# A macaron decoder block on one core: the order of each engine's instructions from the other of two scheduling models

## Chip, core and metric

The kernel runs on one NeuronCore of a Trainium2 chip. The metric is device time in microseconds of one launch; lower is better. A core has five instruction streams that run side by side and wait for each other through semaphores: PE (TensorE, matmuls), DVE (VectorE), ACT (ScalarE), POOL (GpSimd) and SP (SyncE, which only issues DMA transfers here). Each engine takes its own stream strictly in the order in which it was written into the program, so an instruction that waits holds up everything behind it on its engine.

## What is computed

One decoder layer of 1024 tokens and width 1024 in float32: a half-weight SwiGLU feed-forward block of width 2816, a mixer that merges gated linear attention (GLA, 4 heads) with gated DeltaNet (8 heads), and a second such feed-forward block; RMSNorm stands ahead of each and at the end.

```python
h = x
h = h + 0.5 * swiglu(rms_norm(h, ffn1_norm), w_gate1, w_up1, w_down1)
h = h + hybrid_mixer(rms_norm(h, mix_norm), ...)
h = h + 0.5 * swiglu(rms_norm(h, ffn2_norm), w_gate2, w_up2, w_down2)
out = rms_norm(h, final_norm)

# DeltaNet in the mixer, each head, over chunks of the sequence, one after the other:
def step(S, xs):
    qdc, qkc, uc, wc, kc, gc = xs
    v_new = uc - wc @ S
    o = qdc @ S + qkc @ v_new
    S = S * gc + kc.T @ v_new
    return S, o
```

The state S of a DeltaNet head goes from chunk to chunk, so the chunks of a head can't run side by side.

## The kernel before

**Stages.** Activations lie with features on the 128 partitions and the 1024 tokens along the free axis. The stages follow one another: the first feed-forward block (its norm, gate and up products in seven-product block form, then the down products), the mixer's DeltaNet heads, its GLA heads, the output product, the second feed-forward block, the last norm. By the trace the first gate and up products run to about 464 us, the down products to 640, the DeltaNet stage to about 1378, GLA to 1882, the output product and the start of the second feed-forward block to 2026, its gate and up products to 2406, its down products to 2568.

**Matmuls in float32.** Every large product is made of three matmuls on operands split into a high and a low part: high by ACT (a cast, L118 or L124), low by DVE (a subtraction, L119 or L125). `dense` (L137) takes a weight unit times 1024 tokens; `strassen` (L366) and `down` (L572) take block products, and several products accumulate into one PSUM bank, with DVE reading the bank in between (L577 in `down`, L377 in `strassen`).

**The start.** While the first products run, DVE computes the norm's factor ny (L202 to L206), which PE spreads over partitions (L211); and the block sums t2, t3 and t4 of the activations (L320, L327, L329, split at L125), which the fourth and fifth product of a `strassen` call need (L366 on t2h, t2l, t3h, t3l).

**A DeltaNet head.** `delta_rec` runs eight chunk steps, each a chain in which PE and DVE take turns, all on 128 x 128 tiles:

```python
nc.tensor.matmul(out=q[:, :P], lhsT=kT[:, c, :], rhs=S, ...)         # L1013
nc.vector.tensor_sub(out=r, in0=vt3[:, c, :], in1=q[:, :P])          # L1015
nc.tensor.matmul(out=q[:, :P], lhsT=yi3[:, c, :], rhs=r, ...)        # L1017
nc.vector.tensor_scalar(out=w, in0=q[:, :P], scalar1=cj[:, c:c + 1], ...)  # L1019
nc.tensor.matmul(out=oc, lhsT=w, rhs=qk3[:, c, :], ...)              # L1021
nc.tensor.matmul(out=oc, lhsT=S, rhs=qT[:, c, :], ...)               # L1023
nc.tensor.matmul(out=q[:, :P], lhsT=kst3[:, c, :], rhs=w, ...)       # L1026
nc.vector.scalar_tensor_tensor(out=s2, in0=S, scalar=gl[...], in1=q[:, :P], ...)  # L1031
```

After every fourth chunk the output is normed: ACT squares it (L1036), DVE adds (L1037), PE sums over partitions (L799), ACT takes a logarithm, an exponential and a square (L801 to L803, with two table loads), DVE finishes (L804, L805, L1039). Behind the last chunk of a head stands what the next head needs before its first L1017: transposes (L875), the products of k and q (L901), transposes of v (L962), and the levels of a blocked inverse (L980, L993), which PE, ACT and DVE take in turns; all read and write the four PSUM banks named q. Ahead of that, GpSimd has solved small triangles (L923, L926), and DMAs bring them back in blocks, xb and yb (L932 and in `delta_blocks`).

The projections of later heads (`project` through `dense`, L137, 128 x 512) are independent of this chain; each head brings 144 of them or more.

**What sets the order.** The program text only lists instructions and their data. At the end of the `with tile.TileContext(nc) as tc:` block the library's scheduler lays every engine's instructions out in a list of its own choice. It walks through the program with a timing model of the engines and places, at each point, what the model holds to be ready. The text gives it hints: `tc.high_priority(offset=400)` lifts an instruction ahead of others, `tc.issue_after(x)` keeps it behind x, and buffer counts of pools and PSUM banks bound how far ahead it may go.

Of the kernel before, what the change touches and what calls it, by code (L numbers as in the profile page):

```python
# [48 lines left out]
def tile_macaron_hybrid(  # L49
# [17 lines left out]
    nc = tc.nc  # L67
# [55 lines left out]
    def split(src, hi, lo, eng=None):  # L123
        a = nc.scalar.copy(out=hi, in_=src)  # L124
        b = (eng or nc.vector).tensor_sub(out=lo, in0=src, in1=hi.bitcast(F32))  # L125
        return a.ins, b.ins
# [134 lines left out]
    def block_units(blocks):  # L261
        base, units = 0, []
        for b in blocks:
            nd = 8 // len(b)
            units.append([(base + i, i * nd, nd) for i in range(KT // nd)])
            base += KT // nd
        return units
# [41 lines left out]
    def strassen_products(tp, xs, tmp, corner, raws, place=bank, pool_steps=3):  # L309
        comb = {}  # L310

        def tile512(n):
            return tp.tile([P, 512], F32, name=n, tag=n)

        def sums_own():
            for c in ("t2", "t3", "t4"):
                comb[c] = [tp.tile([P, 4, 512], F32R, name=c + p, tag=c + p) for p in "hl"]
            for k in range(4):
                def join(out, r, sl, eng):
                    eng.tensor_add(out=out, in0=xs[r][0][:, sl].bitcast(F32), in1=xs[r][1][:, sl].bitcast(F32))  # L320
                    return out

                b12 = join(corner(), k, HI, nc.vector)
                b22 = join(tile512("c11"), k + 4, HI, nc.vector)
                b11 = join(tile512("c21"), k, LO, nc.vector)
                b21 = join(tile512("c22"), k + 4, LO, nc.gpsimd)
                nc.vector.tensor_sub(out=b22, in0=b22, in1=b12)  # L327
                split(b22, *(x[:, k] for x in comb["t3"]))
                nc.vector.tensor_add(out=b11, in0=b11, in1=b22)  # L329
                split(b11, *(x[:, k] for x in comb["t2"]))  # L330
                nc.gpsimd.tensor_sub(out=b21, in0=b21, in1=b11)
                split(b21, *(x[:, k] for x in comb["t4"]), nc.gpsimd)

        def sums_inplace(k, tile):
            eng = nc.gpsimd if k < pool_steps else nc.vector
            hi, lo = xs[k][0][:, HI], xs[k][1][:, HI]
            v = tile(eng)
            eng.tensor_add(out=v, in0=lo.bitcast(F32), in1=hi.bitcast(F32))
            for t in xs[k]:
                eng.tensor_sub(out=v, in0=v, in1=t[:, LO].bitcast(F32))  # L340
            split(v, hi, lo, eng)

        def strassen(u0, u1, out, mid=None, early=False, begin=(None, None), last_sb=False):
            # Two weight units times x as a 2 x 2 block product (units x features, features x tokens) in the seven
            # products of Winograd's form of Strassen's scheme; those that follow one another in an output
            # accumulate in one bank. The sums of blocks are float32, split into hi and lo like any operand.
            srcs = ((u0, 0), (u0, 1), (u1, 0), (u1, 1))
            a11, a12, a21, a22 = raws()
            for t, (u, hf) in zip((a11, a12, a21, a22), srcs):
                nc.sync.dma_start(out=t, in_=u[:, hf * 512:hf * 512 + 512])  # L350

            def combine(o, a, b, op):
                with tc.high_priority(offset=400), tc.issue_after(norm_end[0]):
                    nc.gpsimd.tensor_tensor(out=o, in0=a, in1=b, op=op)  # L354
                return o

            def product(ps, w, xpart, first=False):
                wh = wp.tile([P, 512], F32R, name="wh", tag="wh")
                wl = wp.tile([P, 512], F32R, name="wl", tag="wl")
                with tc.high_priority(offset=400):  # L360
                    recent[:] = split(w, wh, wl)
                for k in range(4):
                    c = slice(k * P, k * P + P)
                    xh, xl = xpart(k)
                    for a, (p, q) in enumerate(((wh, xl), (wl, xh), (wh, xh))):
                        nc.tensor.matmul(out=ps, lhsT=p[:, c], rhs=q, start=(first and k == 0 and a == 0),  # L366
                                         stop=(k == 3 and a == 2), skip_group_check=not first)

            def keep(name, ps):
                t = tile512(name)  # L370
                with tc.high_priority(offset=400):
                    marks[0] = nc.scalar.copy(out=t, in_=ps).ins  # L372
                return t

            def add(t, ps):
                with tc.high_priority(offset=400):
                    marks[1] = nc.vector.tensor_add(out=t, in0=t, in1=ps).ins  # L377
                return t

            def part(r, sl):  # L380
                return lambda k: [t[:, sl] for t in xs[r + k]]

            def own(c):
                return lambda k: [t[:, k] for t in comb[c]]

            marks = [None, None]
            y = place()
            product(y, a11, part(0, LO), True)
            if begin[0]:
                begin[0]()  # L390
            c11 = keep("c11", y)
            q = place()
            product(q, a12, part(4, LO), True)
            if begin[1]:
                begin[1]()
            add(c11, q)
            out(0, LO, c11, q)
            s1 = combine(tmp(), a21, a22, ALU.add)
            combine(a21, a11, a21, ALU.subtract)
            combine(a11, s1, a11, ALU.subtract)  # L400
            combine(a12, a12, a11, ALU.subtract)
            if mid and early:
                mid(marks)
            product(y, a11, own("t2"))
            c21 = keep("c21", y)
            z = place()
            product(z, a21, own("t3"), True)
            c22 = keep("c22", z)
            if mid and not early:
                mid(marks)  # L410
            product(y, s1, part(0, HI))
            out(1, HI, add(c22, y), c22)
            product(z, a22, own("t4"))
            out(1, LO, add(c21, z), c21)
            product(y, a12, part(4, HI))
            if last_sb:
                out(0, HI, keep("c11", y), None)
            else:
                out(0, HI, y, tile512("c11"))

        return sums_own, sums_inplace, strassen
# [281 lines left out]
    with ExitStack() as st:  # L703
# [7 lines left out]
        units = block_units(OBLOCKS)[1]  # L711
# [733 lines left out]
```

## Time and profile before

| | |
|---|---|
| time, median of 3 | 2680.55 us (2671.61 to 2687.12) |
| span of the profiled execution | 2675.6 us |
| PE busy | 2510.3 us, 94% |
| DVE busy | 1871.0 us, 70% |
| ACT, POOL busy | 1066.7 and 1070.4 us, 40% each |
| mean granted clock of TensorE | 0.979 |

No separate time is listed for the profiled execution: its span, from first to last instruction, is 4.95 us below the median and stands for it. "Busy" of PE overlaps: a lone matmul is counted with its whole latency, so PE can look busier than the work it has. In the rows of single instructions the columns are start, duration, engine, line, operation, and result <- operands with shapes; a bracket at the end gives the idle time before the row and what ended it. [...]

### The profile page before, as it was taken

To read this page: it belongs to the slowest core of one execution; us is meant where nothing else is said; L and a number is where in the kernel's file an instruction comes from. 1 tells how busy PE (TensorE), PEld (TensorE's weight loads), DVE (VectorE), ACT (ScalarE), POOL (GpSimd) and SP (SyncE) were. 2 spreads that over 40 slices of the span, in tenths; PEclk is the share of its full clock that TensorE was granted. 3 is DMA by queue.
4 is the path that set the end of the run, shared out by engine and by line. 5 is a ranking of instruction groups with operands and counts; after the bars stand their busy time and mean duration, and the time that the engine had idled before them with its cause. 6 is when DMAs were issued, how large, how long until landed. Compare 5 with 4: busy or idle time off the path is not lost.

```text
span 2675.6 us, 32736 instructions
## 1 busy us (share of the span) xinstructions
PE 2510.3 (94%) x11656; PEld 2021.6 (76%) x11656; DVE 1871.0 (70%) x2907; ACT 1066.7 (40%) x1845; POOL 1070.4 (40%) x1136
## 2 busy tenths in 40 slices
PE   7899999899997998889989999999989999998998
PEld 6788888667776777767767787877768888886677
DVE  8755556999686777766596757767586555559996
ACT  5333334333352444444344544535233333343331
POOL 4544444653326344443352212221144544446531
PEclk9999999999998999999999999999999999999999
DMA  3222221322221222222211212122302222213222
GB/s 113 79 74 80 83 91 60 114 79 90 95 82 47 64 60 60 56 52 52 64 50 41 80 44 79 43 80 87 122 29 78 68 87 87 87 59 114 79 87 79
DMA packets 150819, 199.05 MB, mean 74 GB/s; under 512 B 69976, under 2 KB 76888, under 8 KB 150656
## 3 DMA queue, kind: packets, MB, share of 16 engines
q1 hardware_dynamic: 146192, 186.14, 22.0%
q0 software_dynamic: 2304, 8.39, 0.8%
q10 hardware_dynamic: 2160, 2.43, 0.3%
q8 instruction: 92, 1.51, 0.2%
q14 instruction: 71, 0.58, 0.1%
HBM read 158.73 MB, written 38.17 MB: 74 GB/s over the span
## 4 chain that ended last, share of the span: by engine, by line
PE 58%; DVE 16%; POOL 11%; issue 5%; ACT 4%; DMA 4%; SPq 2%; POOLq 0%; DVEq 0%; ACTq 0%
PE q L366 28%; PE m L366 10%; PE ps L137 8%; PE q L572 6%; POOL xp L926 5%; POOL itmp L923 4%; DVE wl L125 2%; DVE ha L577 1%; PE q L901 1%; DVE xl L125 1%; DMA lt<-l_d 1%; DVE h L577 1%; DMA raw<-in_win 1%; DMA s<-a_d 1%; SPq L932 1%
## 5 line engine op out<-in xcount | busy, mean ns | idle before, releaser
L125 DVE TENSOR_TENSOR wl<-raw,wh 128x512 fp32r<-128x512 f32 x244 | 199.7, 819 | 172.0 <-ACT wh L124 170.5
L137 PE MATMUL ps<-xl,wh 128*128 128x512 f32 (+2 forms) x736 | 256.8, 408 | 20.5 <-ACT wh L118 8.2
L125 DVE TENSOR_TENSOR wl<-sr,wh 128x512 fp32r<-128x512 f32 x232 | 204.1, 880 | 77.0 <-ACT wh L124 76.7
L137 PE MATMUL ps<-xh,wh 128*128 128x512 f32 (+2 forms) x736 | 254.4, 405 | 0.0
L137 PE MATMUL ps<-xh,wl 128*128 128x512 f32 (+2 forms) x736 | 254.1, 404 | 0.1
L366 PE MATMUL q<-xh,wl 128*128 128x512 f32 x640 | 250.0, 391 | 0.0
L366 PE MATMUL q<-xl,wh 128*128 128x512 f32 x640 | 249.4, 390 | 0.0
L366 PE MATMUL q<-xh,wh 128*128 128x512 f32 x640 | 249.0, 389 | 0.0
L124 ACT CAST wh<-sr 128x512 fp32r<-128x512 f32 x232 | 143.7, 619 | 244.2 <-PE q L572 62.1
L923 POOL TENSOR_TENSOR itmp<-lt,xp 128x112 f32<-128x112 f32 (+29 forms) x248 | 114.2, 461 | 292.7 <-DMA lt<-l_d 273.9
L124 ACT CAST wh<-raw 128x512 fp32r<-128x512 f32 x244 | 144.9, 594 | 175.7 <-PE q L366 101.0
L471 POOL TENSOR_TENSOR s<-s,ysc 128x512 f32<-128x512 f32 x80 | 112.2, 1414 | 248.0 <-ACT s L470 248.0
L137 PEld LDWEIGHTS ps<-xl,wh 128*128 128x128 f32 (+1 forms) x736 | 137.9, 192 | 51.1 <-DVE xl L237 9.0
L354 POOL TENSOR_TENSOR raw<-sr 128x512 f32<-128x512 f32 x20 | 26.4, 1322 | 331.3 <-DMA sr<-in_win 218.0
L137 PEld LDWEIGHTS ps<-xh,wl 128*128 128x128 f32 (+1 forms) x736 | 138.8, 192 | 24.6 <-issue 1.0
L137 PEld LDWEIGHTS ps<-xh,wh 128*128 128x128 f32 (+1 forms) x736 | 138.0, 192 | 24.4 <-issue 1.0
L377 DVE TENSOR_TENSOR c<-c,q 128x512 f32<-128x512 f32 x120 | 82.4, 687 | 85.4 <-PE q L366 85.4
L366 PEld LDWEIGHTS q<-xl,wh 128*128 128x128 f32 x640 | 120.1, 188 | 26.8 <-issue 0.3
L366 PEld LDWEIGHTS q<-xh,wl 128*128 128x128 f32 x640 | 120.1, 188 | 25.6
L366 PEld LDWEIGHTS q<-xh,wh 128*128 128x128 f32 x640 | 120.2, 188 | 25.5
L372 ACT COPY c<-q 128x512 f32<-128x512 f32 x120 | 70.3, 586 | 163.0 <-PE q L366 162.8
L926 POOL TENSOR_TENSOR xp<-xp,itmp 128x112 f32<-128x112 f32 (+29 forms) x248 | 120.3, 485 | 19.4
(481 smaller groups left out, 6742.9 us busy)
## 6 DMA issues: line engine op xcount, KB each, us to landing
sr<-in_win SPq DMA_DIRECT2D x80, 256.0 KB, 2.6
a_d<-s SPq DMA_DIRECT2D x36, 512.0 KB, 3.6
raw<-in_win SPq DMA_DIRECT2D x66, 256.0 KB, 2.7
raw<-in_d SPq DMA_DIRECT2D x56, 256.0 KB, 2.6
raw<-in_g SPq DMA_DIRECT2D x48, 256.0 KB, 2.6
s<-a_d SPq DMA_DIRECT2D x24, 512.0 KB, 4.2
sr<-in_u SPq DMA_DIRECT2D x44, 256.0 KB, 2.7
raw<-in_u SPq DMA_DIRECT2D x44, 256.0 KB, 2.6
```

The source lines that it names most:

```text
L124: a = nc.scalar.copy(out=hi, in_=src)
L125: b = (eng or nc.vector).tensor_sub(out=lo, in0=src, in1=hi.bitcast(F32))
L137: mm = nc.tensor.matmul(out=ps[:m, sl], lhsT=w[:, :m], rhs=x[:, sl], start=(i == 0 and a == 0), stop=(i == n - 1 and a == 2))
L366: nc.tensor.matmul(out=ps, lhsT=p[:, c], rhs=q, start=(first and k == 0 and a == 0), stop=(k == 3 and a == 2), skip_group_check=not first)
L372: marks[0] = nc.scalar.copy(out=t, in_=ps).ins
L377: marks[1] = nc.vector.tensor_add(out=t, in0=t, in1=ps).ins
L471: nc.gpsimd.tensor_mul(out=s, in0=s, in1=y)
L572: nc.tensor.matmul(out=ps, lhsT=p[:, c], rhs=q, start=(first and k == 0 and a == 0), stop=(k == 1 and a == 2), skip_group_check=not first)
L577: nc.vector.scalar_tensor_tensor(out=hd[:, sl], in0=ps, scalar=0.5, in1=hd[:, sl], op0=ALU.mult, op1=ALU.add)
L901: nc.tensor.matmul(out=q[:, n * 256:n * 256 + 256], lhsT=kT[:, c, :], rhs=kq[:, c, :, :], start=True, stop=True)
L923: inv_eng.tensor_tensor(out=tv, in0=lp[:, j, j + 1:].unsqueeze(2).broadcast_to([P, r, m]), in1=xp[:, j, :m].unsqueeze(1).broadcast_to([P, ...
L926: inv_eng.tensor_tensor(out=xv, in0=xv, in1=tv, op=ALU.subtract)
```

## The change

The context that holds the whole kernel gets one more argument, so that the scheduler uses the library's other timing model for its decisions. Three comment lines in `strassen` are blanked.

```diff
         def strassen(u0, u1, out, mid=None, early=False, begin=(None, None), last_sb=False):
-            # Two weight units times x as a 2 x 2 block product (units x features, features x tokens) in the seven
-            # products of Winograd's form of Strassen's scheme; those that follow one another in an output
-            # accumulate in one bank. The sums of blocks are float32, split into hi and lo like any operand.
+
+
+
             srcs = ((u0, 0), (u0, 1), (u1, 0), (u1, 1))
...
-    with tile.TileContext(nc) as tc:
+    with tile.TileContext(nc, schedule_with_timeline_sim=True) as tc:
         tile_macaron_hybrid(tc, *args)
```

The instructions are the same on every engine; their order differs, and table loads stand at other places. On PE, the gate and up stages differ by neighbouring products that change places; most of the movement is in the DeltaNet stage. Three places follow, before and then now; a number behind an underscore is a buffer's.

PE, the chunk steps of the third head in the order of before (`L137` on ps_8360 and ps_8578 are projections of later heads):

```order
L1026 MATMUL q_8121<-rw_8112,kst0_6986 128x128
L137 MATMUL ps_8360<-xh5_5443,wl_8370 128x512
L137 MATMUL ps_8360<-xh5_5443,wh_8369 128x512 x2
L137 MATMUL ps_8360<-xl6_5449,wh_8369 128x512
L1013 MATMUL q_8126<-S_8123,kq2_6591 128x128
L137 MATMUL ps_8360<-xl6_5449,wh_8369 128x512
L137 MATMUL ps_8360<-xh6_5448,wl_8370 128x512 x2
L1017 MATMUL q_8129<-rw_8125,yi_8008 128x128
L137 MATMUL ps_8360<-xh6_5448,wh_8369 128x512 x2
L137 MATMUL ps_8360<-xl7_5454,wh_8369 128x512 x2
L137 MATMUL ps_8360<-xh7_5453,wl_8370 128x512
L1021 MATMUL q_8089<-qk0_7034,rw_8125 128x128
```

PE, the same chunk steps now, from the last projection ahead of them on:

```order
L137 MATMUL ps_8875<-xh7_5453,wh_8884 128x512 x2
L1013 MATMUL q_8113<-S_8110,kq2_6591 128x128
L1017 MATMUL q_8116<-rw_8112,yi_8008 128x128
L1021 MATMUL q_8089<-qk0_7034,rw_8112 128x128
L1023 MATMUL q_8089<-kq2_6591,S_8110 128x128
L1026 MATMUL q_8121<-rw_8112,kst0_6986 128x128
L1013 MATMUL q_8126<-S_8123,kq2_6591 128x128
L1017 MATMUL q_8129<-rw_8125,yi_8008 128x128
L1021 MATMUL q_8089<-qk0_7034,rw_8125 128x128
L1023 MATMUL q_8089<-kq2_6591,S_8123 128x128
L1026 MATMUL q_8134<-rw_8125,kst0_6986 128x128
L799 MATMUL q_8141<-h_8138,cs_67 128x512
```

Where three to five projection matmuls stood between two steps of the chain, none stands now; the projections stand in lumps of 18 to 24 between the steps of the first chunks of the head and inside the last levels behind it.

DVE at the same place, around the first L804 of the head, before:

```order
L1015 TENSOR_TENSOR rw_8152<-vt_7697,q_8153 128x128
L790 SCALAR_TENSOR_TENSOR acc_8561<-ps_8360,ph_5772,acc_8561 128x510
L1019 TENSOR_SCALAR rw_8152<-q_8156,cj_7030 128x128
L790 SCALAR_TENSOR_TENSOR acc_8561<-ps_8360,ph_5772,acc_8561 128x509
L1031 SCALAR_TENSOR_TENSOR S_8163<-S_8136,glast_6974,q_8161 128x128
L1015 TENSOR_TENSOR rw_8165<-vt_7697,q_8166 128x128
L1019 TENSOR_SCALAR rw_8165<-q_8169,cj_7030 128x128
L953 SCALAR_TENSOR_TENSOR acc_8561<-sig_8566,acc_8561 128x512
L804 SCALAR_TENSOR_TENSOR h_8143<-q_8141,h_8143 128x512
```

and now:

```order
L1015 TENSOR_TENSOR rw_8152<-vt_7697,q_8153 128x128
L1019 TENSOR_SCALAR rw_8152<-q_8156,cj_7030 128x128
L804 SCALAR_TENSOR_TENSOR h_8143<-q_8141,h_8143 128x512
L1031 SCALAR_TENSOR_TENSOR S_8163<-S_8136,glast_6974,q_8161 128x128
L805 SCALAR_TENSOR_TENSOR h_8144<-h_8143,h_8144 128x512
```

L804, which needs ACT's L803, has moved ahead of the L1031 and the two steps behind it, which stood ahead of it before.

ACT ahead of the squares of the same head, before (L118 casts weights of later projections):

```order
L118 CAST wh_9025<-raw_9023 128x512
L850 ACTIVATE glast_8298<-glast_8298 128x8
L794 ACTIVATE sig_8574<-acc_8569 128x512
L863 ACTIVATE gb_8290<-gb_8290 128x1024
L1036 ACTIVATE h_8200<-q_8151 128x512
L118 CAST wh_9031<-raw_9029 128x512
L966 ACTIVATE qsq_8645<-kq0_7253 128x1024
```

and now:

```order
L118 CAST wh_9025<-raw_9023 128x512
L794 ACTIVATE sig_8574<-acc_8569 128x512
L118 CAST wh_9031<-raw_9029 128x512
L118 CAST wh_9243<-raw_9241 128x512
L118 CAST wh_9249<-raw_9247 128x512
L1036 ACTIVATE h_8138<-q_8089 128x512
```

The cast wh_9031 has moved from behind the head's second square (h_8200) to ahead of its first (h_8138).

## Rows read from the trace of the kernel before

**Rows 1.** The page's head: span, then busy time and share of each engine.

```profile
span 2675.6 us, 32736 instructions
PE 2510.3 (94%) x11656; PEld 2021.6 (76%) x11656; DVE 1871.0 (70%) x2907; ACT 1066.7 (40%) x1845; POOL 1070.4 (40%) x1136
```

**Rows 2.** Busy time by stretch: start, first gate and up, both down stages.

```profile
0.00:85.45 85.45, 60.97 (x313) 50.71 (x313) 77.98 (x91) 41.49 (x74) 49.24 (x34) 0.95 0.29 98
85.45:464.00 378.55, 378.55 (x1635) 308.06 (x1636) 213.29 (x287) 140.49 (x244) 168.08 (x117) 0.99 0.24 79
464.00:640.00 176.00, 158.85 (x657) 120.34 (x656) 165.38 (x217) 67.33 (x117) 102.08 (x90) 1.00 0.30 99
...
2406.00:2568.00 162.00, 146.03 (x598) 110.61 (x596) 150.78 (x197) 60.40 (x108) 94.60 (x83) 0.99 0.29 96
```

**Rows 3.** Waits of PE: waiting line <- what ended it: total us, times, longest.

```profile
PE q L901 <- DVE h L804: 30.3, 5, 8.5
PE q L980 <- DMA xb<-x_d: 13.3, 1, 13.3
PE q L572 <- DVE ha L577: 13.0, 14, 2.9
PE q L572 <- DVE h L577: 12.2, 14, 2.3
PE q L211 <- DVE ny L206: 12.2, 7, 5.7
...
PE q L366 <- ACT c L372: 8.4, 1, 8.4
...
PE q L1017 <- DVE rw L1015: 4.9, 7, 1.0
PE q L799 <- DVE h L1037: 4.6, 3, 3.8
...
PE q L1013 <- DVE S L1031: 3.3, 3, 2.5
```

**Rows 4.** Instructions of PE in one chunk step of the third head.

```profile
1006.58 0.39 PE L1013 MATMUL q<-S,kq 128*128 128x128 f32 x2
...
1007.04 0.63 PE L137 MATMUL ps<-xh,wl 128*128 128x512 f32 x2
1007.51 0.38 PE L1017 MATMUL q<-rw,yi 128*128 128x128 f32 x2
...
1008.42 0.40 PE L1021 MATMUL q<-qk,rw 128*128 128x128 f32 x2
...
1008.88 0.39 PE L1026 MATMUL q<-rw,kst 128*128 128x128 f32 x2
...
1010.04 0.38 PE L1013 MATMUL q<-S,kq 128*128 128x128 f32 x2
```

**Rows 5.** PE's first L799 of that head, and ACT's L803 behind it.

```profile
1002.18 1.09 PE L799 MATMUL q<-h,cs 128*128 128x512 f32 x2
...
1007.17 0.61 ACT L803 ACTIVATE h<-h 128x512 f32<-128x512 f32 x1
```

**Rows 6.** PE from the last chunk of that head to the next head.

```profile
1016.04 0.39 PE L1023 MATMUL q<-kq,S 128*128 128x128 f32 x2
...
1018.56 1.02 PE L799 MATMUL q<-h,cs 128*128 128x512 f32 x2
...
1030.17 3.78 PE L901 MATMUL q<-kq 128*128 128x256 f32 x8 [6.05 <-DVE h L804]
...
1056.48 0.49 PE L1017 MATMUL q<-vt,yi 128*128 128x128 f32 x2
```

**Rows 7.** ACT in that stretch: the weight cast it waits for.

```profile
1022.93 0.62 ACT L118 CAST wh<-raw 128x512 fp32r<-128x512 f32 x1 [5.31 <-DMA raw<-in_win]
```

**Rows 8.** Short stretches with their granted clock (column ahead of the last two).

```profile
1368.00:1371.40 3.40, 2.33 (x13) 1.67 (x12) 3.40 (x3) 0.35 (x1) 3.40 (x3) 1.00 0.02 5
1029.30:1036.20 6.90, 6.03 (x14) 4.85 (x15) 4.52 (x13) 2.39 (x14) 0.00 (x0) 0.51 0.31 128
```

## The prediction

> **What bounds the kernel now.** I read the page's head first: PE is busy for 94% of the span and no other engine for more than 70% [rows 1]. So the time is PE's work plus PE's idle time, and a new order can only change the idle time: the instructions are the same. Next come the stretches. In the gate and up products PE is busy for all of 378.55 us [rows 2]; products that change places there have nothing to give and, with work queued on both sides, nothing to lose. Then PE's waits [rows 3]: the largest are 30.3 us of L901 for DVE's L804, 13.3 us of L980 for the DMA that brings xb, 25.2 us in the two down stages (13.0 and 12.2), 12.2 us of L211 for the norm and 8.4 us of the first product that needs the sums t2. These are what a better order could save. Last I looked at where PE does not wait although its work is a chain: the DeltaNet chunk steps. One chunk takes 1010.04 - 1006.58 = 3.46 us [rows 4], and in it there is no idle time in the timeline, because three to five projection matmuls lie in each turn. The three small waits of the chain over all eight heads come to only 4.9 + 4.6 + 3.3 = 12.8 us [rows 3]. So the projections pay for the chain there; that cover is what this change moves.
>
> **The bare chain.** A turn is PE's step, DVE's answer and PE's next step. L1013 to L1017 takes 1007.51 - 1006.58 = 0.93 us, L1017 to L1021 0.91, and L1026 to the next L1013 1010.04 - 1008.88 = 1.16 with filler that ran over [rows 4]. Over all 176 turns the shortest is 0.92, whatever lies in between, so I take 0.92 as the turn's own length. Of that PE works 0.22 on its own step (L1021 to L1026 are two such steps in 0.46 us). The rest, 0.70 us, is free for others: three projection matmuls at 0.23 each (two in 1007.51 - 1007.04 = 0.47, rows 4). In the new order I counted the turns with nothing in between: 139 of 176, none before. The lumps of 18 to 24 matmuls (4 to 5.5 us) fill one turn each and overflow it; the overflow is work that is done anyway. So 139 x 0.70 = **97 us** of idle time that was covered and is not any more.
>
> **The norm in mid-head.** After the fourth chunk L799 stands in PE's stream behind ACT's L1036 and DVE's L1037. At the end of the head L799 starts 1018.56 - 1016.04 = 2.5 us after the last L1023 [rows 6]. Bare, that is some 1.7 us of PE idle beyond L1026's own 0.22 and what the fourth chunk's turn holds already. Seven heads have that place bare: 7 x 1.7 = **12 us** (0 to 16).
>
> **DVE's L804 in the chain.** DVE now has L804 ahead of the L1031 that closes the next chunk. L804 needs L803, which ends 1007.17 + 0.61 - 1002.18 = 5.6 us after L799's start [rows 5], two table loads included. L1031 would be due about 0.85 (L799's length to the next step) + 0.92 + 0.92 + 0.46 + 0.4 = 3.55 us after it. DVE stands still for up to 2 us and then works 0.69 on L804; what hides it before is that L804 stands two steps later. If the first table load runs ahead of L799, 1.3 us less. I take 2.0 per head, 8 x 2.0 = **16 us** (0 to 22).
>
> **The head's tail.** From the last L1023 to the next head's L1017 there are 1056.48 - 1016.04 = 40.4 us, 56 projection matmuls (12.7 us) and 6.05 + 0.73 us of idle time in it [rows 6]. The 6.05 us come from ACT: L801 to L803 are held up behind the weight cast that waits 5.31 us for its DMA [rows 7]. Now that cast and two more stand ahead of the head's first square, behind the lumps of projections, and I take this hold-up as gone. But from L1023 to the last L980s no projection is left either: the L799 wait (2.5 us), the three ACT steps with their loads (5.6 us) until L901 has a free bank, and the DVE chain from L875 to L962 stand bare. Of the 12.7 us of filler two level waits keep about 2. So between -6.05 (only the hold-up counts) and +10.7 (all filler is exposed) per head; I take the middle, +3 for seven heads = **+21 us** (-42 to +75).
>
> **What goes in the same stage.** 35 us of PE's work now stand ahead of the first head's chain: the 13.3 us wait for xb is covered, **-13**. The 12.8 us of waits in the steps that exist already are contained in the new turns, **-13**. The sum for DeltaNet is 97 + 12 + 16 + 21 - 13 - 13 = **+120 us**.
>
> **The clock.** After idle stretches the granted clock is half: 0.51 over 1029.30 to 1036.20, behind the 6.05 us gap [rows 8]. But a stretch with PE busy for 2.33 of 3.40 us, close to what a bare chain gives (five steps of 0.39 in 3.2 us), had 1.00 [rows 8]. I take **+10 us**, for bare tails in which PE waits longer than now; the case of a clock that falls in the chain itself is a rival below.
>
> **The start.** DVE is busy for 77.98 of the first 85.45 us [rows 2], so it bounds this stage and the order can't shorten its list. ny of the second half stands 13 instructions later than before, at a mean of 77.98/91 = 0.86 us some 11 us; 17 rows of PE's stream have moved ahead of the L211 that needs it and hide about 5. Of the remaining 6 us part comes back, as the 8.4 us wait [rows 3] falls due after it and DVE has the sums done by then: **+5 us** (-8 if that wait goes altogether, +12).
>
> **The down stages.** The matmuls of a bank's next product stood directly behind its last one, with 1.4 us (median) of PE's work between them; now other products lie in between, 4.1 us. That is enough for L577 to be done and would remove the 25.2 us of waits. But DVE is busy for 165.38 of 176.00 and 150.78 of 162.00 us [rows 2]: only 21.8 us are to be had before DVE is the bound, and a stage never gets all. **-10 us** (-22 to +10).
>
> **The second feed-forward block's start.** L211 stands 5 to 6 us of PE's work later and waits up to 5.7 us now [rows 3]: **-5 us** (-8 to +3). The gate and up stages, GLA and the output product I cost at nothing: their waits are small (GLA within +-10), PE has work queued on both sides of each exchange.
>
> Sum: 120 + 10 + 5 - 10 - 5 = +120 us. On the span, 2675.6 + 120 = 2795.6; the median lies 4.95 above the span, so 2800.5.
>
> **Rivals.**
> *Faster: the longer look-ahead wins.* If a bare turn cost little, what remains is the waits that go: 13.3 + 30.3 + 8.4 + 12.2 + 25.2 + 12.8 = 102 us at most; with two thirds of it the time is about 2615. For it speaks that the order stretches just these distances. It decides at the turn's price: 139 turns x 0.49 us = 68 us, so a turn would have to be 0.22 + 0.49 = 0.71 us or less. Against it: no turn in the trace is under 0.92. Chance 0.07.
> *No change.* The bare turns cost 97 + 12, but every wait of L901 (30), xb (13), the steps (13) and about 50 of the other 46 + 10 go as well and DVE never stands at L804: about 2680. It needs all at once; 0.05.
> *A smaller loss.* The turns cost what they must, the tails are no worse than before and DVE's L804 finds ACT done: 97 + 12 - 26 - 20 = +63 with the gains outside full, plus half of the tails: about 2735. Chance 0.13.
> *The clock falls in the bare chain.* Then PE's own steps double (0.22 to 0.44) and the turn grows by about 0.3: 139 x 0.3 = 42 us, and the tails' 15 us of PE work per head at half speed give some 30 more: about 2865. Rows 8 show both levels at a similar share of busy time, one behind a long gap and one not. [...] Chance 0.20.
> *The change does nothing.* Excluded: the orders differ as shown.
>
> **How the numbers follow.** The forecast, 2800.5 us with its own range of 2755 to 2845 (tails and L804 at their bounds, not all at once), has 0.55. The range of 8 in 10 takes in the smaller loss and the clock's case to its centre and a little beyond: 2720 to 2880. Faster than 0.5% 0.07, within 0.5% 0.05, slower by more 0.55 + 0.20 + 0.13 = 0.88; 0.5%, some 13 us, is about what a measurement of this kernel can tell from no change.
>
> **What would show it.** In the changed kernel's timeline the chunk steps stand alone, a chunk takes about 3.2 us with some 2.1 us of idle time ended by L1015, L1019 and L1031, and these three releasers come to about 97 us in PE's waits, where 13 stand now. L980 for xb is gone from the list, L572's waits are shorter, L211's too at 2000 us. A head from L1017 to L1017 takes near 87 us instead of 70. The granted clock in 900 to 1400 us says which clock case holds. I am wrong if a chunk with nothing in it takes well under 3 us, if PE fetches work past a waiting step, or if the gate and up stages, taken as neutral, show waits.

## The result and the profile after

The changed kernel takes 2889.44 us (median of four runs, 2886.33 to 2891.17) where the kernel before, measured a fourth time with it, takes 2678.8: a ratio of 1.0786, 95% interval 1.077 to 1.0802. It is slower by 7.9%, about 211 us; the forecast was 2800.5 us, range 2720 to 2880. The direction and the stage were right, the size was not: of the 211 us the forecast had 120, and the measured time lies above its range.

The page's head of the changed kernel, and the line of the granted clock in 40 equal slices (6 means 0.6 of full speed), against [rows 1]:

```profile
span 2889.2 us, 32734 instructions
...
PE 2628.6 (91%) x11656; PEld 2118.6 (73%) x11656; DVE 1866.0 (65%) x2907; ACT 1069.4 (37%) x1845; POOL 1072.4 (37%) x1136
...
PEclk9999999999996886788877799999999999999999
```

The span grew by 213.6 us. PE's busy time, as the profile counts it, grew by 118.3 us with the same 11656 instructions; only 95.3 us are more idle time. The slices say where the same instructions took longer: in eleven slices, those of the DeltaNet stage, the clock stood at 0.6 to 0.8.

PE's longest waits after, in the form of [rows 3]:

```profile
PE q L1021 <- DVE rw L1019: 31.2, 52, 2.6
PE q L1013 <- DVE S L1031: 28.6, 35, 3.4
PE q L1017 <- DVE rw L1015: 27.4, 49, 4.6
PE q L799 <- DVE h L1037: 19.8, 16, 1.4
PE q L572 <- DVE wl L125: 16.0, 8, 2.7
PE q L901 <- DVE h L804: 16.0, 6, 2.7
PE ps L137 <- DVE xl L237: 14.3, 5, 10.5
PE q L211 <- DVE ny L206: 12.3, 4, 6.8
PE q L962 <- DVE em L907: 10.8, 5, 2.9
...
PE q L980 <- DMA xb<-x_d: 2.8, 1, 2.8
```

The first three rows are PE's waits for DVE inside the chain (L1019, L1031 and L1015 release PE there): 87.2 us together. The wait for xb fell from 13.3 to 2.8, L901's from 30.3 to 16.0.

The next rows are PE in the third head, to be read against [rows 4]. A turn is bare when no projection stands between its two steps. First come the first bare turns behind a lump, then a whole bare chunk:

```profile
1085.39 0.38 PE L1013 MATMUL q<-S,kq 128*128 128x128 f32 x2
1086.15 0.49 PE L1017 MATMUL q<-rw,yi 128*128 128x128 f32 x2 [0.38 <-DVE rw L1015]
1088.39 0.49 PE L1021 MATMUL q<-qk,rw 128*128 128x128 f32 x2 [1.75 <-DVE rw L1019]
...
1101.04 0.80 PE L1013 MATMUL q<-S,kq 128*128 128x128 f32 x2 [0.57 <-DVE S L1031]
1102.21 0.80 PE L1017 MATMUL q<-rw,yi 128*128 128x128 f32 x2 [0.38 <-DVE rw L1015]
1103.45 0.80 PE L1021 MATMUL q<-qk,rw 128*128 128x128 f32 x2 [0.44 <-DVE rw L1019]
1104.04 0.63 PE L1023 MATMUL q<-kq,S 128*128 128x128 f32 x2
1104.46 0.63 PE L1026 MATMUL q<-rw,kst 128*128 128x128 f32 x2
1105.54 0.79 PE L1013 MATMUL q<-S,kq 128*128 128x128 f32 x2 [0.44 <-DVE S L1031]
```

The turn from L1013 to L1017 takes 0.76 us right behind the lump and 1.17 us fifteen us later. The chunk takes 4.50 us, and L1013, L1017 and L1021 last 0.80 in it where they lasted 0.38 to 0.40 in [rows 4]. The same head by stretches: the last lumps, the first bare turns, the other bare chunks, the tail, and the lump at the end of the tail. The columns, here and in [rows 2], are the stretch, its length, busy microseconds and instruction counts of PE, PE's weight loads, DVE, ACT and POOL, then the granted clock of TensorE as a share of full speed, the DMA share and GB/s:

```profile
1061.40:1085.40 24.00, 24.00 (x115) 20.07 (x115) 10.80 (x18) 5.01 (x8) 15.04 (x39) 1.00 0.20 39
1085.40:1095.00 9.60, 5.17 (x22) 3.72 (x21) 3.18 (x8) 2.34 (x3) 0.00 (x0) 0.74 0.45 110
1095.00:1113.00 18.00, 13.26 (x38) 8.98 (x38) 6.27 (x16) 4.56 (x7) 0.00 (x0) 0.50 0.00 0
1113.00:1145.00 32.00, 23.44 (x103) 18.61 (x101) 21.42 (x53) 13.46 (x32) 5.18 (x13) 0.67 0.17 54
1145.00:1158.20 13.20, 13.20 (x64) 10.39 (x64) 10.51 (x15) 4.74 (x7) 12.02 (x16) 1.00 0.07 21
```

The clock is 1.00 in the lumps, falls in the 9.6 us behind them (mean 0.74), in which PE's longest wait is the 1.75 us above, and is 0.50 for all of the 18 us after that.

To place the loss I took, stretch by stretch, the time that passed less PE's work (instructions of each form times their pitch, the time from one start to the next, at full clock in the trace of before). What is left is idle time and time lost to a lower clock. "Chain" is from a head's first L1017 to its last L1023, "tail" from there to the next head's first L1017.

| | before | after | difference |
|---|---|---|---|
| up to the first head's chain | | | -5.3 us |
| eight chains | 23.2 | 199.9 | +176.7 us |
| seven tails | 54.6 | 100.3 | +45.7 us |
| behind the last chain | | | -3.5 us |

These add up to the 213.6 us. Outside the chains and tails of the DeltaNet stage the changes come to -8.8 us.

### The profile page after: what moved, and what is told of

Read it like the earlier page. It is cut to its first block, busy times and chain, and to the rows that moved or that the text cites. A ratio compares the mean times of both kernels' runs of the same rounds, so it can differ in the third digit from the quotient of the medians.

```text
span 2889.2 us, 32734 instructions
## 1 busy us (share of the span) xinstructions
PE 2628.6 (91%) x11656; PEld 2118.6 (73%) x11656; DVE 1866.0 (65%) x2907; ACT 1069.4 (37%) x1845; POOL 1072.4 (37%) x1136
## 4 chain that ended last, share of the span: by engine, by line
PE 67%; DVE 17%; ACT 4%; POOL 4%; issue 4%; DMA 2%; SPq 1%; DVEq 0%; POOLq 0%; ACTq 0%
PE q L366 26%; PE ps L137 14%; PE m L366 11%; PE q L572 6%; DVE wl L125 2%; POOL xp L926 2%; PE q L980 2%; DVE xl L125 1%; POOL itmp L923 1%; PE q L1021 1%; PE q L1017 1%; PE q L901 1%; PE q L799 1%; DVE h L577 1%; DVE ha L577 1%
## 5 line engine op out<-in xcount | busy, mean ns | idle before, releaser
L125 DVE TENSOR_TENSOR wl<-raw,wh 128x512 fp32r<-128x512 f32 x244 | 226.9, 930 | 166.1 <-ACT wh L124 165.0
L137 PE MATMUL ps<-xl,wh 128*128 128x512 f32 (+2 forms) x736 | 242.7, 398 | 27.5 <-DVE xl L237 14.3
L366 PE MATMUL q<-xh,wh 128*128 128x512 f32 x640 | 242.8, 389 | 0.0
L137 PE MATMUL ps<-xh,wl 128*128 128x512 f32 (+2 forms) x736 | 240.9, 394 | 0.1
L137 PE MATMUL ps<-xh,wh 128*128 128x512 f32 (+2 forms) x736 | 240.5, 393 | 0.0
L125 DVE TENSOR_TENSOR wl<-sr,wh 128x512 fp32r<-128x512 f32 x232 | 177.3, 765 | 59.3 <-ACT wh L124 57.9
L471 POOL TENSOR_TENSOR s<-s,ysc 128x512 f32<-128x512 f32 x80 | 104.0, 1300 | 294.8 <-ACT s L470 294.8
L124 ACT CAST wh<-raw 128x512 fp32r<-128x512 f32 x244 | 144.5, 593 | 177.2 <-PE q L366 61.8
L137 PEld LDWEIGHTS ps<-xl,wh 128*128 128x128 f32 (+1 forms) x736 | 138.4, 191 | 61.2 <-ACT wh L118 10.5
L137 PEld LDWEIGHTS ps<-xh,wl 128*128 128x128 f32 (+1 forms) x736 | 140.3, 191 | 28.9 <-DVE wl L119 0.4
L137 PEld LDWEIGHTS ps<-xh,wh 128*128 128x128 f32 (+1 forms) x736 | 140.1, 191 | 29.0 <-issue 0.7
L366 PE MATMUL m<-xl,wh 128*128 128x512 f32 x320 | 129.6, 408 | 9.9 <-DVE c L377 5.1
L118 ACT CAST wh<-raw 128x512 fp32r<-128x512 f32 x94 | 58.1, 619 | 203.1 <-PE ps L137 137.9
L366 PE MATMUL m<-xh,wl 128*128 128x512 f32 x320 | 126.8, 396 | 0.0
```

The costliest lines, as they stand in the source:

```text
L118: nc.scalar.copy(out=wh, in_=raw)
L137: mm = nc.tensor.matmul(out=ps[:m, sl], lhsT=w[:, :m], rhs=x[:, sl], start=(i == 0 and a == 0), stop=(i == n - 1 and a == 2))
L471: nc.gpsimd.tensor_mul(out=s, in0=s, in1=y)
```

## The experiments

**PE's order alone, in both directions.** The scheduler keeps its model, but instructions of one engine are tied to each other in a given order (issue order only, no wait). The diffs of this section show the lines that matter; a remark behind a # tells what stands elsewhere in the kernel. The list holds the 2328 PE instructions of the DeltaNet stage:

```diff
     with tile.TileContext(nc, schedule_with_timeline_sim=True) as tc:
         tile_macaron_hybrid(tc, *args)
+        pin_order(tc, ORDER_PE)   # for each neighbouring pair a, b: tc.add_manual_dep(b, a, NoSync)
```

Changed kernel with the PE order of before:

> The other timing model stays, but PE's 2328 instructions of the DeltaNet stage (those that ran from 735 to 1380 us in the kernel before) are pinned to each other in the order of before; every other engine and every other stage keeps what the scheduler makes of it. Theory 1 (the loss comes from PE's bare chunk steps, their idle turns and the half clock that follows): the heads go back to about 70 us each and the time to 2678.8 + 7 (what the start and the first down stage lost) - 5 (second feed-forward start) plus or minus 15, so 2665 to 2700. Rival (the loss comes from what DVE, ACT and SP were given: L804 ahead of L1031, casts ahead of the squares): at most half of the 211 us comes back, 2780 or more.

Measured 2683.15 us, ratio to before 1.0028 (1.0018 to 1.0038), clock 0.98: the loss is gone, as theory 1 had it. Kernel before with the PE order of the changed kernel:

> The timing model of before, but the same 2328 PE instructions pinned in the order of the changed kernel. Theory 1: nearly all of the loss of the DeltaNet stage (211 us) appears, 2860 to 2900. Rival (other engines' order): 2680 to 2780.

Measured 2920.0 us, ratio 1.0919 (1.0901 to 1.0937), clock 0.927. So PE's order in this stage carries the whole loss, under either model. The second time is 20 us above the range: with this PE order, the other engines' order of before gives a time some 31 us longer than the order that belongs to it.

With PE's order back, the chains took 294 us over eight heads (249 before) and the tails 242 (278 before). In the chains, DVE's stream is the suspect; DVE first, then PE, in that kernel:

```profile
1015.47 0.69 DVE L804 SCALAR_TENSOR_TENSOR h<-q,h 128x512 f32<-128x512 f32 x1 [1.92 <-ACT h L803]
...
1016.47 0.49 PE L1013 MATMUL q<-S,kq 128*128 128x128 f32 x2 [1.66 <-DVE S L1031]
```

L804 waits 1.92 us for ACT with the chain's L1031 behind it, and PE waits 1.66 us, although projections stand in the turn.

**Holding the clock.** Matmuls that nobody reads are put into the bare turns, into columns of the PSUM bank that the chain step leaves unused, so that PE has more to do in time in which it would wait:

```diff
-                q = bank()
-                nc.tensor.matmul(out=q[:, :P], lhsT=yi3[:, c, :], rhs=r, start=True, stop=True)
+                q = hold(nc, xs, bank())   # n matmuls: out=q[:, P:], lhsT=xs[0][0][:, :P], rhs=xs[0][0][:, P:512]
+                held(nc.tensor.matmul(out=q[:, :P], lhsT=yi3[:, c, :], rhs=r, start=True, stop=True))
```

and the same ahead of L1013 and of L1021 (but for L1021 of a head's last chunk). With three:

> The changed kernel, its PE order of the DeltaNet stage pinned, with three matmuls of 384 columns added ahead of each L1013, L1017 and L1021, whose result nobody reads; they depend on nothing of the turn and lie in its idle time (about 0.17 us each, 0.5 of the 0.7 us). They add 552 matmuls, some 95 us of PE work. Theory 1a (half of the loss is the half clock in the bare chain): the clock stays at 1.00 there, a bare chunk goes from 4.5 to about 3.2 us, and the kernel gets faster although it does more: 8 heads x 5.5 chunks x 1.3 = 57 us less, plus up to 25 for tails that begin at full clock, minus 18 for turns that are filled already: 2810 to 2850. Theory 1b (the idle turns themselves are the loss, the clock is a bystander): no gain, 2890 to 2930.

Measured 2869.71 us, ratio 1.0728 (1.0712 to 1.0744), mean clock 0.969 instead of 0.927. With one:

> As the kernel with three added matmuls ahead of each L1013, L1017 and L1021, but with one (0.17 us of the 0.7). Theory 1a: if this is enough to hold the clock, 2805 to 2850 too; if it isn't, the added work runs at half clock inside the turns and the time stays at 2880 to 2900. Theory 1b: 2885 to 2900.

Measured 2888.9 us, ratio 1.0796 (1.078 to 1.0813), clock 0.94. With one the clock was 0.51 over 1110 to 1130 us and 0.82 over 880 to 1380 us, where the changed kernel has 0.77, and the time is that of the changed kernel. With three it was 0.93 over 880 to 1380 us and 20 us came back although PE had 528 instructions more. That lies between what the two theories expected: the tails grew by 13 us, the order of DVE and ACT not being pinned, and turns that held projections got added matmuls too. So the same was done only in the bare turns and with every engine's order pinned:

> The changed kernel again with three added matmuls (384 columns, nobody reads the result), now only ahead of those L1013, L1017 and L1021 that stand bare, and with all five engines' order of the DeltaNet stage pinned as in the changed kernel, so that nothing else can move. In the kernel with three added matmuls everywhere a bare chunk took 3.18 us at clock 1.00 instead of 4.50, but tails grew by 13 us and filled turns by about 18. Theory: the half clock costs 53 bare chunks x 1.3 = 70 us less what L804's wait takes back (8 heads x 1 to 2 us), and the tails don't depend on it: 2820 to 2845. Rival: the clock buys nothing because the tails and L804 wait for ACT and take it back: 2865 to 2890.

Measured 2842.57 us, ratio 1.0609 (1.0588 to 1.063): 47 us faster than the changed kernel, with more work; in the traces the order of PE, DVE and ACT is the same in both. PE in a bare chunk of it (L1471 are the added matmuls), then the clock of the stretch:

```profile
1086.53 0.49 PE L1013 MATMUL q<-S,kq 128*128 128x128 f32 x2
1086.77 0.77 PE L1471 MATMUL q<-xh 128*128 128x384 f32 x3
1087.39 0.49 PE L1017 MATMUL q<-rw,yi 128*128 128x128 f32 x2
...
1088.33 0.49 PE L1021 MATMUL q<-qk,rw 128*128 128x128 f32 x2
...
1088.88 0.39 PE L1026 MATMUL q<-rw,kst 128*128 128x128 f32 x2
...
1089.70 0.49 PE L1013 MATMUL q<-S,kq 128*128 128x128 f32 x2
...
1090.84 0.49 PE L1017 MATMUL q<-rw,yi 128*128 128x128 f32 x2
1091.77 0.49 PE L1021 MATMUL q<-qk,rw 128*128 128x128 f32 x2 [0.45 <-DVE rw L1019]
```

```profile
1080.00:1095.00 15.00, 11.91 (x67) 9.01 (x67) 6.60 (x17) 4.96 (x8) 0.00 (x0) 1.00 0.01 2
```

The chunk takes 3.17 us at 1.00 where it took 4.50 at 0.50. The chains went from 398.7 to 364.3 us, and the tails, which the expectation took as independent of it, from 323.0 to 312.3. The last two rows are a turn left bare, 0.93 us at 1.00. The 47 us are a lower bound for what the clock costs: in places it still fell (0.66 over 1071 to 1076 us, behind a wait of 1.71 us), and L901's waits for L804 in the tails grew from 16.0 to 23.2 us.

**DVE back as well.**

> The other timing model with PE and DVE both pinned to their DeltaNet order of before; ACT, SP and POOL keep the new order. With PE alone pinned the chains took 294 us over eight heads (before: 249) because DVE's L804 and weight subtractions stood ahead of chain steps, and the tails 242 us (before: 278) because no L901 waits behind a weight cast. If those two are DVE's and ACT's order respectively, the chains go back to about 250 and the tails stay near 245: 2683 - 40 = 2635 to 2655, faster than both kernels. Rival: ACT's casts are what lengthens the chains: 2675 to 2690.

```diff
+        pin_order(tc, ORDERS)   # the lists of PE and of DVE (962 instructions), DeltaNet stage, order of before
```

Measured 2658.89 us, ratio 0.9922 (0.9898 to 0.9947): 0.8% faster than the kernel before, 4 us above the range. The chains are back at 248.6 us, so their lengthening with PE's order alone back was DVE's order, and not ACT's casts. The tails are at 261.4, not 245: L901 now waits 11.0 us for L1039, a little further on in DVE's stream, and 7.7 for L804.

**One cast later.** That L901's wait in [rows 6, 7] is the weight cast's doing can be tried in the kernel before by moving five casts alone:

> The kernel before, its own timing model and its own orders of PE, DVE and ACT in the DeltaNet stage pinned, with one thing moved: in the five heads where L901 waits for L804 (30.3 us), the weight cast that stands ahead of L801 on ACT and waits for its DMA, and its subtraction on DVE, go behind L803 and L805. If the hold-up is the cast, L901's waits fall to about 5 us and the time to 2675 - 20 to 25 = 2645 to 2660. Rival: the projections that need the cast come late instead and the time stays at 2670 to 2680.

```diff
+        pin_order(tc, ORDERS)   # PE, DVE, ACT as before; in 5 heads L118's cast behind L803, its L119 behind L805
```

Measured 2659.37 us, ratio 0.9932 (0.9908 to 0.9956). ACT, then PE, at the place of [rows 7]:

```profile
1018.65 1.28 ACT L801 ACT_TABLE_LOAD   x1
1019.94 0.60 ACT L801 ACTIVATE h<-q 128x512 f32<-128x512 f32 x1
...
1022.90 0.62 ACT L803 ACTIVATE h<-h 128x512 f32<-128x512 f32 x1
1023.42 0.60 ACT L118 CAST wh<-raw 128x512 fp32r<-128x512 f32 x1
...
1024.29 2.31 PE L901 MATMUL q<-kq 128*128 128x256 f32 x8 [0.96 <-DVE h L804]
```

The cast comes behind L803 and holds nothing up; L901's wait is 0.96 us instead of 6.05. Over the five heads L901's waits for L804 fall from 30.3 to 4.6 us, but 10.2 us of waits for L1039, which stands behind it on DVE, take their place. The tails fall from 277.6 to 261.2 us, the chains stay at 249.0. The gain, 20 us, is about that of the experiment before it, with the order of the old timing model; whether both gains are the same waits was not tried.

## Why the prediction missed

- **What bounds the kernel: right.** PE's work is the same, and only its idle time and its speed moved. I compared the start of PE's instruction number n in both traces. Through the first gate and up products the changed kernel is 2.7 us late, neither more nor less (forecast for the start: 5); the start of the second feed-forward block takes 4.5 us back (216.0 to 211.5 us late, forecast 5), and the second gate and up products keep the 211.5. So these products were neutral, as taken.
- **The clock: the step that failed.** The prediction put +10 us for it, on one stretch of [rows 8] that was busy for 2.33 of 3.40 us and stood at 1.00, and gave the falling clock a chance of 0.20 with 2865 us. That reading was wrong in two ways. Seven projections lay in the stretch, so it was no bare chain; and in the same trace the clock fell right behind it, after a wait of 2.48 us:

```profile
1371.40:1374.80 3.40, 1.56 (x7) 1.09 (x7) 3.40 (x5) 0.60 (x1) 3.40 (x3) 0.89 0.00 0
1374.80:1378.20 3.40, 3.40 (x13) 2.82 (x13) 3.11 (x5) 0.26 (x2) 0.65 (x2) 0.60 0.00 0
```

  Nor are the two stretches of [rows 8] busy for a similar share: 0.69 at 1.00 and 0.87 at 0.51. In the changed kernel 113 of the 139 bare turns had a mean clock of 0.55 or less, 18 one of 0.95 or more. Holding the clock by added work gave 47 us back, and a chunk went from 4.50 to 3.17 us. Counted by the length of turns (below), the clock costs some 59 us in the chains, and the tails were 11 us shorter with the clock held: about 70 us, an estimate, instead of 10. In the third head the clock fell between small idles (up to 1.75 us ahead of the fall shown) and stayed at 0.50 for the 18 us shown. Whether the idle time or the small amount of PE work between it brings the clock down was not separated: the added matmuls change both.
- **The bare turn: near, with a wrong reason.** The prediction took 0.92 us as a turn's own length, "whatever lies in between". In the kernel before, a turn takes 0.92 us with three projections in it, 1.15 with four and 1.39 with five (medians): that is PE's own work, 0.22 + 0.23 for each. Bare and at full clock L1013 to L1017 takes 0.87 us (0.76 right behind a lump), L1017 to L1021 0.93 and L1026 to L1013 0.83. Less PE's own 0.22 these make 92 us over 139 turns; forecast 97.
- **The chains' 176.7 us by the turns of the changed kernel.** At 0.50 the same three turns take 1.17, 1.24 and 1.07 us (medians). A bare turn that is longer than its kind at its clock was held up by DVE. This is worked out from the trace, to about 5 us a line:

| | forecast | from the trace |
|---|---|---|
| bare turns at full clock; L1021 to L1026, 6 us longer when bare | 97 | 98 us |
| lower clock: in bare turns 34, from L1021 to L1026 18, at the norm 7 | 10 | 59 us |
| bare turns held up by DVE | 16 | 28 us |
| norm in mid-head | 12 | 10 us |
| what the chains of before lost and these do not | -13 | -18 us |
| sum | 122 | 177 us |

- **DVE's L804 in the chain: right mechanism, half the size.** DVE's 2902 instructions (memsets not counted) started in the order of its list in both traces, so an L1031 behind L804 waits with it. Forecast 2.0 us per head, 16 in all. In five heads the bare turn in which DVE runs L804 ahead of L1031 (in four of them L805 and L1039 too) is 0.85 to 2.75 us longer than its kind, 8.6 us together; in the third head it is 1.21 us against 1.07.
- **What the prediction left out in the chain: other work of DVE.** In four heads a weight subtraction L119, which waits for ACT's cast, stands ahead of a chain step, 6 us together. ACT, then DVE, in the changed kernel:

```profile
1086.73 0.62 ACT L118 CAST wh<-raw 128x512 fp32r<-128x512 f32 x1 [6.65 <-PE q L1017]
...
1087.38 0.69 DVE L119 TENSOR_TENSOR wl<-raw,wh 128x512 fp32r<-128x512 f32 x1 [1.28 <-ACT wh L118]
1087.99 0.35 DVE L1019 TENSOR_SCALAR rw<-q,cj 128x128 f32<-128x128 f32 x1
```

  L1017 started at 1086.15 and L1021 at 1088.39: the turn took 2.24 us, 1.3 more than its kind. In the last head block sums (L320, L327, L329 and their split L125) add 12 us. The kernel before has such a loss there too (its last chain takes 42.9 us, the others 28.9 to 30.6), which is most of the 18 us in the table.
- **The tails: mis-sized.** +45.7 us against +21 (bounds -42 to +75); the middle of the prediction's bounds for a head, -6.05 and +10.7, is 2.3 and not 3, which would have made 16. Some 11 us are the clock (323.0 against 312.3 us with the clock held). The hold-up behind the weight cast is gone, but L901's waits fell by 14 us only, from 30.3 to 16.0: L901 still waits for the norm's steps, which stand bare. The filler that went covered more than I took: L799, L901 and L962 wait one after the other. How the other 35 us split was not tried.
- **The down stages: mis-sized, small.** L577's waits fell from 25.2 to 10.8 us, but L572 now waits 16.0 us for the weights' subtraction L125. By PE's instruction number the two stages took back some 2 us each, 4 instead of 10: the work that came in between had its own operands still to be made. Behind the second one, up to the end, 4 us were lost again.
- **The sum.** Forecast for the chains with the clock 122, measured 176.7; tails 21 against 45.7; the rest -13 + 5 - 10 - 5 = -23, measured -5.3 - 3.5 = -8.8. The misses are 55, 25 and 14 us, 94 together. By the table the clock is 49 of the 55 and DVE 12, less 6 in the other lines; it is 11 of the tails' 25. So some 60 of the 94 us are the clock. One sum among the rivals is loose as well: "a smaller loss" comes to 2680.5 + 63 = 2743.5 us, and half of the tails' +21 would raise it, so 2735 does not follow.

## What to carry to other kernels

Filler (independent work between the steps of a dependent chain) did two things here: it used the idle turns, and with it the granted clock stayed up (0.96 over 880 to 1380 us, 0.77 in the changed kernel). When an order takes it away, price both: the idle time of each bare turn, and the same instructions at a lower clock (here a bare chunk took 4.50 us at 0.50, and 3.17 us at 1.00 with added matmuls in its turns). Read the rows behind a stretch as well as the stretch before you conclude that the clock holds (here 1.00, then 0.89 and 0.60 in the trace of before). And read an order on every engine: PE's order lost 211 us here, while one hold-up on ACT, a weight cast ahead of the norm's steps, was worth 20 us in the kernel before and could be removed alone.

## What the runs showed of the hardware that I had not expected

- The clock of TensorE stood at 0.50 for 18 us in which PE's longest idle time was 0.57 us and its busy time, as counted, 13.26 of 18.00 us. Over 880 to 1380 us it was 0.77 in the changed kernel, 0.82 with one added matmul per turn and 0.93 with three.
- A bare turn PE, DVE, PE on 128 x 128 took 0.76 to 0.93 us at clock 1.00 and 1.07 to 1.24 us at 0.50 (by kind of turn; at 0.50 the medians), where nothing else held DVE up.
- Adding PE work made the kernel faster by 47 us (2889.44 to 2842.57).
